# Strassen operands of the gates queued behind the last head's norm, two pools that wait tile by tile, one sum on another engine, three tiles in other rooms

## The chip, the cores and the metric

The kernel runs on one core of one Trainium2 chip. The metric is the device time of one execution in microseconds (us). TensorE (PE) does the matmuls and the transposes, VectorE (DVE), ScalarE (ACT) and GpSimd (POOL) work on tiles beside it, SyncE (SP) issues most of the DMAs and ACT the rest. Each engine takes its instructions in a fixed order; a wait of one instruction holds everything behind it on that engine, and that goes for SP's DMAs too.

## The reference

One layer of an encoder over 1024 tokens of width 1024, in float32, cut to what matters here:

```python
h = rmsnorm(x, g_mix)
z = h @ w_in                              # pooling channels | q | k | v
y_pool = pool_mixer(u_pool, ...)          # four windows
y_attn = diff_attention(q, k, v, ...)     # 8 heads, two softmax maps each, then
                                          # o = head_rmsnorm(o, g_sub) * (1 - lambda_init)
gates = sigmoid(h @ w_gate + b_gate)      # 2 x 1024 columns
merged = gates[..., :D] * (y_pool @ w_branch_pool) + gates[..., D:] * (y_attn @ w_branch_attn)
x = x + merged @ w_out
h2 = rmsnorm(x, g_ffn)
x = x + square(relu(h2 @ w_up)) @ w_down
```

## The kernel before

Every float32 matmul is done as three matmuls (`mm3`) of operands that are split in a high and a low part of fp32r. `split` makes the two parts: a cast on ACT (L116) and a subtraction on DVE or POOL (L117). Most matmuls are 128x128 by 128x512.

**Order.** The program is written tile by tile, and a planner with a clock of its own puts each engine's instructions in order, those written first going first where several are ready by that clock. `tc.issue_after(ins)` keeps what is written in its block, on the engine of `ins` alone, behind `ins` on that engine; it adds no wait for `ins` to finish. Tiles come from pools; tiles of one tag share the pool's `bufs` rooms in turn. A pool opened where an earlier one lay waits by default until every tile of the earlier ones is done with; with `reuse_waits="tile"` each of its tiles waits for those that lay at its own place.

**The heads.** A pipeline of stages runs over 8 heads with 8 query tiles each. At the end of a head, `stage_norm` makes the row of factors `r` for the head's output norm: three DVE steps (L594 to L596), two on POOL (L597 a power, L598 a product), a transpose on PE (`trr`, L600), a copy on ACT, and a DMA to `r_dram`. Its small tiles lie in the pool `sp`, its PSUM bank in `ps_t`; both close behind the heads, with `ps_s` and `ps_o`.

**Behind the heads** the rest of the mixer follows:

- `vpool` (six rooms of 4 KB a partition, where `sp` lay) and `pb` (five PSUM banks, where `ps_s`, `ps_o` and `ps_t` lay) are opened. `bank` deals the eight PSUM banks in turn: three of `ps_z` and `ps_f`, then five of `pb`.
- The `comb` sums: the token operand `hT` is combined into Strassen-Winograd sums in place, on DVE (L827, L830), and split again.
- `bp`: the pooled branch's projection, 16 groups of 12 matmuls, two for each d; ACT copies each group's bank to `m` (L935), and `m` goes to `mp_dram`.
- `gate_rest(d)` for d from 3 to 7: the rest of the gates' products in Strassen-Winograd form. It is a generator with four steps. Its first step loads `gr` (8 raw tiles of weights) and `ga`, makes S1, S3 and S2 by three POOL sums (L827, L830), splits S2, S1, S3 and A22 on ACT and DVE, and loads `xz`. Its later steps are the products gA and gB. In the second, ACT copies gA to `uv` (L893) before the next product is added to the same bank. In the third, DVE adds A to `v[:, 0]`, POOL adds the two halves of `v` (`xz`, L827), and SP stores that and `uv` to `g_dram`. `xz` and `uv` share four rooms (tag `fw`).
- `gate_rest(3)` and `gate_rest(4)` take their first step within the bp loop, behind d = 3 and d = 5.
- `load_yT(d)` brings the attention output of head d back from `y_dram` (`ryT`) and its factors from `r_dram` (`rb`), multiplies the two on DVE (L925) and splits the product to `yT`. The rows 0 to 4 use rooms of `vpool`, the rows 5 to 7 the one room of the tag `mx`. `fr` (two rooms of 2 KB) holds the gates' raw operand `ga`, and later sums (`tmp`).
- `ba`: the attention branch's projection, over all eight `yT`; then the gates, the output projection and the second norm.

**The MLP.** Up: 16 pairs of column blocks, seven Strassen-Winograd products each (`up_pair`). X is a PSUM bank in which product 6 is followed by product 7, added to the same bank, so ACT must copy X to `U2` (L1216) between them. `U2` takes one of nine rooms of the pool `e1` (tag `ev`), as do most other results of a pair; these go to DRAM (`ud`) by DMA. The operand sums S1 to S4 take rooms of the tag `sm`, in `es`, `e20` or `e21` by the pair's number. Down: seven products (Da, Db) with operands read back from DRAM; the rooms of its weight loads lie, among others, where `pr21` and `e21` lay.

Of the kernel before, what the change touches and what calls it, by code (L numbers as in the profile page):

```python
# [54 lines left out]
def encoder_kernel(  # L55
# [58 lines left out]
    def split(hi, lo, src, lo_eng=None):  # L114

        nc.scalar.copy(hi, src)  # L116
        return (lo_eng or nc.vector).tensor_tensor(lo, src, f(hi), op=ALU.subtract)  # L117
# [17 lines left out]
    def fr_tile(shape, name):  # L135
        return fp.tile(shape, F32, tag="fr", name=name, bufs=N_FR)
# [136 lines left out]
    with ExitStack() as ph:  # L273
# [116 lines left out]
        Zs = {}  # L390
        SS = {}

        gghs, z_last = {}, {}


        sq = sp.tile([P, 4, HD + 1], F32, name="sq")
# [192 lines left out]
        def stage_norm(h):  # L589

            rz = sp.tile([P, NT], F32, tag="rz", name=f"rz{h}")
            r = sp.tile([P, NT], F32, tag="r", name=f"r{h}")
            nc.vector.reciprocal(rz, Zs[h][:, 0, :])
            nc.vector.tensor_tensor(r, SS[h], rz, op=ALU.mult)  # L594
            nc.vector.tensor_tensor(r, r, rz, op=ALU.mult)
            nc.vector.tensor_scalar(r, r, 1.0 / P, EPS, op0=ALU.mult, op1=ALU.add)  # L596
            nc.gpsimd.tensor_tensor(r, r, mhalf, op=ALU.pow)  # L597
            nc.gpsimd.tensor_tensor(r, r, rz, op=ALU.mult)  # L598
            tr = ps_t.tile([P, 512], F32, tag="tr", name=f"trr{h}")
            nc.tensor.transpose(tr[0:NT, 0:P], r, identf)  # L600
            rT = sp.tile([NT, P], F32, tag="rT", name=f"rT{h}")
            nc.scalar.copy(rT, tr[0:NT, 0:P])
            nc.scalar.dma_start(r_dram[h].rearrange("(t q) -> t q", q=P), rT)
            yield
# [191 lines left out]
        next(gen)  # L796


    vpool = attn.enter_context(tc.tile_pool(name="vpool", bufs=N_V))
    pb = mix.enter_context(tc.tile_pool(name="pb", bufs=5, space=PSUM))  # L800
    nbank = [0]

    def vt(shape, dt, name):
        return vpool.tile(shape, dt, tag="V", name=name)
# [21 lines left out]
    def add(eng, out_, a, b):  # L826
        return eng.tensor_tensor(out_, a, b, op=ALU.add)  # L827
# [44 lines left out]
    def gate_rest(d):  # L872
        ds_ = slice(d * P, (d + 1) * P)
        r2 = raw([P, NK, P], f"gr{d}")
        nc.sync.dma_start(r2, w_gate[:, D + d * P : D + (d + 1) * P].rearrange("(kk p) c -> p kk c", p=P))
        r21, r22 = r2[:, 0:4, :], r2[:, 4:8, :]
        r11 = gate_raw(11, d)
        s1 = fo_tile(f"s1_{d}")[:, 0:512].rearrange("p (a b) -> p a b", a=4)
        add(pool, s1, r21, r22)
        sub(pool, r21, r11, r21)  # L880
        sub(pool, r11, s1, r11)
        ws = []
        for name, rw in (("S2", r11), ("S1", s1), ("S3", r21), ("A22", r22)):
            w = wt([P, 2, 4, P], f"{name}_{d}")
            split_made[d] = split(w[:, 0], w[:, 1], rw)
            ws.append(w)
        v = fw_tile([P, 2, 512], f"xz{d}", F32)
        nc.sync.dma_start(v, xz[ds_])
        u = fw_tile([P, 2, 512], f"uv{d}", F32)
        yield  # L890
        A, B = bank(f"gA_{d}"), bank(f"gB_{d}")
        gate_mm(A, ws[0], 2, True, True)
        nc.scalar.copy(u[:, 0, :], A)  # L893
        add(dve, u[:, 0, :], u[:, 0, :], v[:, 0, :])
        yield
        gate_mm(B, ws[2], 3, True, True)
        nc.scalar.copy(u[:, 1, :], B)
        gate_mm(A, ws[1], 1, False, True, True)
        add(dve, v[:, 0, :], A, v[:, 0, :])
        add(pool, v[:, 1, :], v[:, 0, :], v[:, 1, :])  # L900
        nc.sync.dma_start(g_dram[ds_, 512:S], v[:, 1, :])
        add(dve, u[:, 1, :], u[:, 1, :], v[:, 0, :])
        nc.sync.dma_start(g_dram[D + d * P : D + (d + 1) * P, 512:S], u[:, 1, :])
        yield
        gate_mm(B, ws[3], 4, False, True, True)
        add(dve, u[:, 0, :], B, u[:, 0, :])
        nc.sync.dma_start(g_dram[D + d * P : D + (d + 1) * P, 0:512], u[:, 0, :])
        yield
# [3 lines left out]
    def load_yT(d):  # L912

        rb = fu_tile(f"rb{d}") if d % 2 else ut([P, S], F32, f"rb{d}")
        nc.sync.dma_start(rb, r_dram[d].partition_broadcast(P))
        if d < N_YU:
            rw = vt([P, S], F32, f"ryT{d}")
        else:
            rw = fq.tile([P, S], F32, tag="mx", name=f"ryT{d}")
        nc.sync.dma_start(rw, y_dram[d * P : (d + 1) * P, :])  # L920
        ts = []
        for th in range(2):
            hs = slice(th * 512, (th + 1) * 512)
            t = yt_tile(d)([P, 2, 512], F32R, f"yT{d}_{th}", th)
            dve.scalar_tensor_tensor(rw[:, hs], rw[:, hs], gs, rb[:, hs], op0=ALU.mult, op1=ALU.mult)  # L925
            split(t[:, 0, :], t[:, 1, :], rw[:, hs])
            ts.append(t)
        yT.append(ts)

    gens = [gate_rest(d) for d in range(G_PLAIN, NK)]  # L930
    for d in range(NK):
        m = ut([P, S], F32, f"m{d}")
        for th in range(2):
            ps = proj_T(bank(f"bp{d}_{th}"), ws_bp[d - d % 2][d % 2], lambda k, th: pair(ypT[k][th]), th, nk=4)
            nc.scalar.copy(m[:, th * 512 : (th + 1) * 512], ps)  # L935
        nc.scalar.dma_start(mp_dram[d * P : (d + 1) * P, :], m)

        if d in (3, 5):
            next(gens[d // 2 - 1])

    NG = len(gens)
    for i in range(NG + 1):
# [167 lines left out]
    def ev(name, shape=(P, 512)):  # L1110
        return e1.tile(list(shape), F32, tag="ev", name=name)
# [62 lines left out]
    def up_pair(p):  # L1174
        cols_p = w_up[:, p * 2 * P : (p + 1) * 2 * P].rearrange("(kk p) (i c) -> i p kk c", p=P, i=2)

        def load(i, pool_):
            r = pool_.tile([P, NK, P], F32, tag="rw", name=f"wu{p}_{i}")
            nc.sync.dma_start(r, cols_p[i])
            return {f"{i + 1}{j + 1}": r[:, 4 * j : 4 * j + 4, :] for j in range(2)}  # L1180

        A = load(0, pr1)
        X = bx.tile([P, 512], F32, tag="X", name=f"X{p}", bufs=4)
        Y = (bm if p % 2 else bx).tile([P, 512], F32, tag="Y", name=f"Y{p}")
        u_product(X, "1", a_op(p, "11", A["11"], dve))
# [12 lines left out]
        def store(name, src, queue=nc.sync):  # L1198
            queue.dma_start(ud[name, p // 2][:, p % 2, :], src)

        finish("11", Y, x1)
        store("11", C["11"], nc.scalar)
        yield
        A.update(load(1, pr2[p % 3 > 0]))
        yield
        S1, S2, S3, S4 = (
            (e2[1] if p % 3 and p != 1 else e2[0] if i > 2 else es).tile(
                [P, 4, P], F32, tag="sm", name=f"s{i}_{p}"
            )
            for i in range(1, 5)  # L1210
        )
        add(dve, S1, A["21"], A["22"])
        sub(dve, S2, S1, A["11"])
        u_product(X, "6", a_op(p, "S2", S2, dve))
        U2 = ev(f"U2_{p}")
        nc.scalar.copy(U2, X)  # L1216
        zp, zt, zb = (bx, "X", 4) if p % 2 else (bm, "Z", 1)
        Z = zp.tile([P, 512], F32, tag=zt, name=f"Z{p}", bufs=zb)
        u_product(Z, "5", a_op(p, "S1", S1, dve))
        z5 = ev(f"z5_{p}")  # L1220
        nc.scalar.copy(z5, Z)
        sub(dve, S3, A["11"], A["21"])
        u_product(X, "7", a_op(p, "S3", S3, dve))
        U3 = ev(f"U3_{p}")
        nc.scalar.copy(U3, X)
        finish("22", X, z5)
        store("22", C["22"], nc.scalar)
        W = bm.tile([P, 512], F32, tag="W", name=f"W{p}")
        u_product(W, "4", a_op(p, "22", A["22"], dve))
        finish("21", W, U3)  # L1230
        store("12", C["21"], nc.scalar)
        sub(dve, S4, A["12"], S2)
        u_product(Z, "3", a_op(p, "S4", S4, dve))
        finish("12", Z, U2)

        s1 = ev(f"us1_{p}")
        add(dve, s1, C["12"], C["22"])
        store("S1", s1)
        s2 = ev(f"us2_{p}")
        sub(dve, s2, s1, C["11"])  # L1240
# [224 lines left out]
```

## Time and profile before

| | before |
|---|---|
| median of 3 runs | 1565.0 us (1563.77 to 1567.16) |
| the profiled execution | 1566.65 us, span 1564.8 us, granted clock 0.996 |
| PE busy | 1534.5 us (98%) |
| DVE, ACT, POOL busy | 992.4, 824.6, 401.5 us |
| DMA | 223.97 MB, mean 143 GB/s |

Rows of a timeline give start and duration in us, engine, line, operation, the tiles written and read with buffer numbers left out, shapes and count; in brackets stands how long the engine sat idle before it and what ended that. PE's ends are modelled, so the pace of matmuls is read from start to start. "PEclk" is the share of the full clock that was granted to PE. In the chain of waits each row is one piece of the work that ended last, and "issue" is time in which nothing that the profile shows was waited for.

### The profile page before, as it was taken

How to read it: one execution, taken by the hardware profiler on the slowest of the kernel's cores; microseconds unless marked ns; L12 is line 12 of the kernel's file. 1: busy time of each engine (PE TensorE's matmuls, PEld its weight loads, DVE VectorE, ACT ScalarE, POOL GpSimd, SP SyncE). 2: the span in 40 equal slices, each digit the busy share in tenths (PEclk: the TensorE clock that was granted, in tenths of full speed). 3: DMA queues.
4: the chain of work that ended last, by engine and by line, in shares of the span. 5: the costliest groups of instructions: out<-in, count | busy, mean ns of one | idle time of the engine just before them, and what ended most of it. 6: DMA issues, size and time to landing. Idle time of an engine off the chain costs nothing.

```text
span 1564.8 us, 21964 instructions
## 1 busy us (share of the span) xinstructions
PE 1534.5 (98%) x7653; PEld 1319.8 (84%) x7653; DVE 992.4 (63%) x1986; ACT 824.6 (53%) x1828; POOL 401.5 (26%) x484
## 2 busy tenths in 40 slices
PE   7999999999999999899999999999999999999998
PEld 6999999989999988777788887888888788888887
DVE  6666677676767765748542448866565668556662
ACT  6656566656576665344442547565555634333331
POOL 5525253535463451315545400000000000000000
PEclk9999999999999999999999999999999999999999
DMA  7202021212131123276766633554342789537650
GB/s 228 63 25 85 32 82 43 71 45 73 49 94 62 58 71 107 90 243 216 274 221 199 197 110 123 187 178 165 128 141 108 275 297 376 194 121 254 223 188 27
DMA packets 177544, 223.97 MB, mean 143 GB/s; under 512 B 10565, under 2 KB 111130, under 8 KB 177434
## 3 DMA queue, kind: packets, MB, share of 16 engines
q1 hardware_dynamic: 159594, 192.39, 37.7%
q10 hardware_dynamic: 17840, 30.19, 5.2%
q8 instruction: 60, 0.98, 0.3%
q14 instruction: 50, 0.41, 0.1%
HBM read 161.16 MB, written 61.37 MB: 142 GB/s over the span
## 4 chain that ended last, share of the span: by engine, by line
PE 85%; DVE 5%; DMA 4%; ACT 2%; issue 1%; POOL 1%; SPq 1%; ACTq 0%; DVEq 0%; POOLq 0%
PE z L122 5%; PE z L123 5%; PE z L124 5%; PE Da L123 4%; PE Da L122 4%; PE Da L124 4%; PE Db L123 3%; PE Db L122 3%; PE Db L124 3%; PE X L124 3%; PE X L122 3%; PE X L123 2%; PE sc L492 2%; PE sc L493 2%; PE op L124 2%; PE op L122 2%
## 5 line engine op out<-in xcount | busy, mean ns | idle before, releaser
L122 PE MATMUL z<-wqkv,hT 128*128 128x384 f32 x512 | 175.2, 343 | 0.3 <-DVE qn L436 0.2
L123 PE MATMUL z<-wqkv,hT 128*128 128x384 f32 x512 | 174.5, 342 | 0.4 <-POOL wqkv L117 0.4
L124 PE MATMUL z<-wqkv,hT 128*128 128x384 f32 x512 | 174.3, 341 | 0.4 <-DVE hT L117 0.3
L503 ACT ACTIVATE s<-s,nm 128x256 f32<-128x256 f32 (+7 forms) x128 | 99.7, 779 | 50.4 <-DVE nm L495 48.2
L433 POOL TENSOR_TENSOR ms<-ms,mhalf 128x4 f32<-128x4 f32 x64 | 68.6, 1073 | 135.2 <-DVE ms L431 135.0
L122 PEld LDWEIGHTS z<-wqkv,hT 128*128 128x128 f32 x512 | 97.1, 190 | 3.4 <-DVE qn L436 0.7
L124 PEld LDWEIGHTS z<-wqkv,hT 128*128 128x128 f32 x512 | 97.0, 190 | 3.5 <-DVE hT L117 1.2
L123 PEld LDWEIGHTS z<-wqkv,hT 128*128 128x128 f32 x512 | 97.2, 190 | 3.2 <-POOL wqkv L117 0.7
L495 DVE CUSTOM_DVE_ANT_0 s<-sc,dist 128x512 f32<-128x512 f32 (+3 forms) x128 | 74.8, 586 | 25.5 <-PE sc L493 22.9
L492 PE MATMUL sc<-K,Q 128*128 128x512 f32 (+2 forms) x192 | 68.5, 361 | 0.9 <-ACT oS L574 0.4
L493 PE MATMUL sc<-K,Q 128*128 128x512 f32 (+2 forms) x192 | 66.8, 355 | 0.0
L117 DVE TENSOR_TENSOR AS<-s,AS 128x512 fp32r<-128x512 f32 x64 | 43.7, 686 | 35.5 <-ACT AS L116 35.3
L117 POOL TENSOR_TENSOR wqkv<-rqkv,wqkv 128x384 fp32r<-128x384 f32 x60 | 62.9, 1067 | 8.8 <-ACT wqkv L116 4.7
L442 POOL TENSOR_TENSOR qn<-qn,ggh 128x128 f32<-128x128 f32 x64 | 31.4, 490 | 86.7 <-DVE qn L436 79.2
L123 PE MATMUL ba<-yT,wba 128*128 128x512 f32 x128 | 50.7, 396 | 1.1 <-DVE yT L117 1.1
L465 DVE TENSOR_TENSOR Q<-tk,Q 64x128 fp32r<-64x128 f32 x128 | 36.6, 286 | 22.7 <-ACT Q L464 20.9
L124 PE MATMUL ba<-yT,wba 128*128 128x512 f32 x128 | 50.6, 395 | 0.0
L122 PE MATMUL ba<-yT,wba 128*128 128x512 f32 x128 | 50.6, 395 | 0.0
L122 PE MATMUL op<-wo,mT 128*128 128x512 f32 x128 | 50.2, 396 | 0.0
L466 ACT CAST Q<-tk 64x128 fp32r<-64x128 f32 x128 | 33.2, 260 | 32.3 <-DVE Q L465 30.1
L123 PE MATMUL op<-wo,mT 128*128 128x512 f32 x128 | 50.2, 394 | 0.0
L124 PE MATMUL op<-wo,mT 128*128 128x512 f32 x128 | 50.1, 393 | 0.0
(489 smaller groups left out, 4796.1 us busy)
## 6 DMA issues: line engine op xcount, KB each, us to landing
wd<-in_w_down_dram SPq DMA_DIRECT2D x56, 512.0 KB, 5.5
wu<-in_w_up_dram SPq DMA_DIRECT2D x32, 512.0 KB, 4.7
udS<-us SPq DMA_DIRECT2D x64, 256.0 KB, 2.1
ur<-udS SPq DMA_DIRECT2D x32, 512.0 KB, 4.0
rqkv<-in_w_in_dram SPq DMA_DIRECT2D x64, 192.0 KB, 2.7
ud<-u ACTq DMA_DIRECT2D x48, 256.0 KB, 2.1
ur<-ud SPq DMA_DIRECT2D x24, 512.0 KB, 4.2
ga<-in_w_gate_dram SPq DMA_DIRECT2D x25, 256.0 KB, 2.8
```

Of the source, the lines that this page charges most:

```text
L117: return (lo_eng or nc.vector).tensor_tensor(lo, src, f(hi), op=ALU.subtract)
L122: nc.tensor.matmul(ps, lhs_hi, rhs_hi, start=first, stop=False, **kw)
L123: nc.tensor.matmul(ps, lhs_hi, rhs_lo, start=False, stop=False, **kw)
L124: return nc.tensor.matmul(ps, lhs_lo, rhs_hi, start=False, stop=last, **kw)
L433: nc.gpsimd.tensor_tensor(ms, ms, mhalf[:, 0:4], op=ALU.pow)
L442: nc.gpsimd.tensor_tensor(qn[:, 2:4, :], qn[:, 2:4, :], ggh.unsqueeze(1).broadcast_to([P, 2, HD]), op=ALU.mult)
L465: nc.vector.tensor_tensor(Q[own, m, 1, :], q, f(q_hi), op=ALU.subtract)
L466: nc.scalar.copy(Q[other, m, 1, :], q)
L492: nc.tensor.matmul(dst, Q[:, i, 0, :], rhs, start=True, stop=False)
L493: nc.tensor.matmul(dst, Q[:, i, 1, :], rhs, start=False, stop=True)
L495: nc.vector.tensor_tensor_reduce(out=s[i][:, c : c + w], in0=sc[:, 0:w], in1=dist[:, o0 + c : o0 + c + w], scale=2.0 ** -(h + 1), scalar=B ...
L503: nc.scalar.activation(s[i][:, 0:n], s[i][:, 0:n], AF.Exp, bias=last, scale=-1.0, accum_out=Z[:, i, t : t + 1])
```

## The change

- The DVE and POOL instructions of the first steps of `gate_rest(3)` and `gate_rest(4)` stand behind the last head's L596 on DVE and its L598 on POOL.
- `vpool` and `pb` wait tile by tile.
- The sum of the two halves of `v` in `gate_rest` runs on DVE.
- `load_yT(7)` loads its row as two halves into the two rooms of `fr`, by two DMAs, in place of the `mx` room.
- `U2` of the last pair (15) takes a room of `e21`, whose tiles were last the operand sums of pair 14.

```diff
-        gghs, z_last = {}, {}
+        gghs, z_last, normed = {}, {}, {}
...
-            nc.vector.tensor_scalar(r, r, 1.0 / P, EPS, op0=ALU.mult, op1=ALU.add)
+            normed[h] = [nc.vector.tensor_scalar(r, r, 1.0 / P, EPS, op0=ALU.mult, op1=ALU.add)]
             nc.gpsimd.tensor_tensor(r, r, mhalf, op=ALU.pow)
-            nc.gpsimd.tensor_tensor(r, r, rz, op=ALU.mult)
+            normed[h].append(nc.gpsimd.tensor_tensor(r, r, rz, op=ALU.mult))
...
-    vpool = attn.enter_context(tc.tile_pool(name="vpool", bufs=N_V))
-    pb = mix.enter_context(tc.tile_pool(name="pb", bufs=5, space=PSUM))
+    vpool = attn.enter_context(tc.tile_pool(name="vpool", bufs=N_V, reuse_waits="tile"))
+    pb = mix.enter_context(tc.tile_pool(name="pb", bufs=5, space=PSUM, reuse_waits="tile"))
...
-        add(pool, v[:, 1, :], v[:, 0, :], v[:, 1, :])
+        add(dve, v[:, 1, :], v[:, 0, :], v[:, 1, :])
...
-        if d < N_YU:
-            rw = vt([P, S], F32, f"ryT{d}")
+        if d == NK - 1:
+
+            rws = [fr_tile([P, 512], f"ryT{d}_{th}") for th in range(2)]
+            for th in range(2):
+                nc.sync.dma_start(rws[th], y_dram[d * P : (d + 1) * P, th * 512 : (th + 1) * 512])
         else:
-            rw = fq.tile([P, S], F32, tag="mx", name=f"ryT{d}")
-        nc.sync.dma_start(rw, y_dram[d * P : (d + 1) * P, :])
+            if d < N_YU:
+                rw = vt([P, S], F32, f"ryT{d}")
+            else:
+                rw = fq.tile([P, S], F32, tag="mx", name=f"ryT{d}")
+            nc.sync.dma_start(rw, y_dram[d * P : (d + 1) * P, :])
+            rws = [rw[:, 0:512], rw[:, 512:S]]
...
         if d in (3, 5):
-            next(gens[d // 2 - 1])
+            with ExitStack() as later:
+                for ins in normed[H - 1]:
+                    later.enter_context(tc.issue_after(ins.ins))
+                next(gens[d // 2 - 1])
...
-        U2 = ev(f"U2_{p}")
+
+        U2 = ev(f"U2_{p}") if p < NP - 1 else e2[1].tile([P, 512], F32, tag="sm", name=f"U2_{p}")
```

More of the change, by code (lines that the diff above doesn't have):

```diff
@@ L915, in load_yT @@
         nc.sync.dma_start(rb, r_dram[d].partition_broadcast(P))
-        if d < N_YU:
-            rw = vt([P, S], F32, f"ryT{d}")
-        else:
-            rw = fq.tile([P, S], F32, tag="mx", name=f"ryT{d}")
-        nc.sync.dma_start(rw, y_dram[d * P : (d + 1) * P, :])
+        if d == NK - 1:
+            rws = [fr_tile([P, 512], f"ryT{d}_{th}") for th in range(2)]
+            for th in range(2):
+                nc.sync.dma_start(rws[th], y_dram[d * P : (d + 1) * P, th * 512 : (th + 1) * 512])
+        else:
+            if d < N_YU:
[4 more added lines that the diff above has]
+            rws = [rw[:, 0:512], rw[:, 512:S]]
         ts = []
-        for th in range(2):
-            hs = slice(th * 512, (th + 1) * 512)
+        for th, r in enumerate(rws):
             t = yt_tile(d)([P, 2, 512], F32R, f"yT{d}_{th}", th)
-            dve.scalar_tensor_tensor(rw[:, hs], rw[:, hs], gs, rb[:, hs], op0=ALU.mult, op1=ALU.mult)
-            split(t[:, 0, :], t[:, 1, :], rw[:, hs])
+            dve.scalar_tensor_tensor(
+                r, r, gs, rb[:, th * 512 : (th + 1) * 512], op0=ALU.mult, op1=ALU.mult
+            )
+            split(t[:, 0, :], t[:, 1, :], r)
             ts.append(t)
```

## The prediction

> **What bounds the kernel now.** I read the page's busy shares first, then TensorE's waits, then the stretches around the longest of them, then single rows. TensorE (PE) is the bound:
>
> ```profile
> span 1564.8 us, 21964 instructions
> PE 1534.5 (98%) x7653; PEld 1319.8 (84%) x7653; DVE 992.4 (63%) x1986; ACT 824.6 (53%) x1828; POOL 401.5 (26%) x484
> ```
>
> The matmuls stay the same, so only PE's 30.3 us of idle and its slow stretches can go. The list of waits says where they are (engine, tile and line that waited, on whom: us in total, times, longest). Besides one at the start, which the diff doesn't touch, these are the long ones:
>
> ```profile
> PE trr L600 <- POOL r L598: 4.0, 1, 4.0
> PE X L122 <- ACT U L1216: 2.5, 2, 1.9
> PE gA L122 <- ACT uv L893: 2.3, 1, 2.3
> PE bp L122 <- ACT m L935: 1.9, 1, 1.9
> ...
> PE ba L123 <- DVE yT L117: 1.1, 1, 1.1
> ```
>
> The diff can reach all five. Two have a tail in the clock. Stretches (length, busy time of PE, PEld, DVE, ACT and POOL with counts, then PEclk, DMA share, GB/s) and PE's rows show it:
>
> ```profile
> 666.60:672.70 6.10, 6.09 (x15) 4.79 (x16) 4.95 (x5) 2.66 (x4) 0.00 (x0) 0.51 0.70 254
> ...
> 1243.80:1249.50 5.70, 3.83 (x10) 2.94 (x10) 4.96 (x6) 4.34 (x6) 0.00 (x0) 0.70 1.04 402
> ```
>
> ```profile
> 665.89 0.37 PE L600 MATMUL trr<-identf,r 128*8 128x128 f32 x1 [3.96 <-POOL r L598]
> 666.61 0.80 PE L122 MATMUL bp<-ypT,wbp 128*128 128x512 f32 x1 [0.34 <-ACT rT L602]
> ...
> 672.65 0.39 PE L124 MATMUL bp<-ypT,wbp 128*128 128x512 f32 x1
> 672.88 0.39 PE L122 MATMUL bp<-ypT,wbp 128*128 128x512 f32 x1
> ```
>
> The full pace is 0.23 us a matmul (672.65 to 672.88). After the last head's norm the clock is 0.51 for 6 us: 6.10 - 15 x 0.23 = 2.7 lost there, on top of 3.96 + 0.34 idle; the norm costs 7.0. In U2's stretch 5.70 - 10 x 0.23 = 3.4 are lost, 1.9 of it the wait and 1.5 the slow clock.
>
> The Trainium skill, "TensorE: Matmul & The Clock Gate", Part 1, has the clock at half after an idle window of about 3.4 us and back after as long a busy one. By that the norm's tail is half of 3.4, an estimate of 1.7, and a stall of 1.9 us has none; the trace disagrees on both (2.7 and 1.5), and the sum below would be 2.5 us less by the rule.
>
> **The change part by part.**
>
> **Operands behind the norm; pools tile by tile.** Why the norm is late:
>
> ```profile
> 650.48 1.27 DVE L594 TENSOR_TENSOR r<-SS,rz 128x8 f32<-128x8 f32 x1
> ...
> 652.81 1.21 DVE L117 TENSOR_TENSOR hT<-combe,hT 128x1024 fp32r<-128x1024 f32 x1
> ...
> 658.37 1.09 DVE L117 TENSOR_TENSOR S<-ga,S 128x512 fp32r<-128x512 f32 x1 [3.15 <-ACT S L116]
> ...
> 662.75 0.16 DVE L596 TENSOR_SCALAR r<-r 128x8 f32<-128x8 f32 x1
> ```
>
> ```profile
> 647.45 4.28 POOL L827 TENSOR_TENSOR s<-gr 128x512 f32<-128x512 f32 x1 [31.71 <-DMA gr<-in_w_gate_dram]
> ...
> 662.98 2.55 POOL L597 TENSOR_TENSOR r<-r,mhalf 128x8 f32<-128x8 f32 x1 [2.38 <-DVE r L596]
> ...
> 685.09 1.43 POOL L827 TENSOR_TENSOR s<-gr 128x512 f32<-128x512 f32 x1 [19.25 <-DMA gr<-in_w_gate_dram]
> ```
>
> ```profile
> 657.72 0.62 ACT L116 CAST S<-ga 128x512 fp32r<-128x512 f32 x1 [6.60 <-POOL ga L830]
> ...
> 658.24 0.58 ACT L935 COPY m<-bp 128x512 f32<-128x512 f32 x1
> ```
>
> GpSimd (POOL) adds gate operands first; ScalarE's (ACT) cast waits 6.60 us for them, with the copy that empties a bp bank right behind it, which is the bp wait; VectorE's (DVE) subtraction waits for the cast, and the norm's L596 stands behind that. The change puts the DVE and POOL instructions of both moved steps behind L596 and L598. How long the chain takes then, and where PE meets it:
>
> ```profile
> L597 POOL TENSOR_TENSOR r<-r,mhalf x8: 1636/1638/2551, 139.5 to 663.0; 128x8 f32<-128x8 f32 x8
> ```
>
> ```profile
> 642.43 0.40 PE L122 MATMUL bp<-ypT,wbp 128*128 128x512 f32 x1
> ```
>
> L594 at 650.5; a small step takes 0.2 where POOL is off (below); with two sums of DVE, 1.2 each (652.81), between dependent steps L595 comes at 653.1 and L596 at 655.7; then 0.2, 1.64 for the power and 0.2: the transpose can run at 657.7. On PE the transpose stands behind six groups of twelve bp matmuls that begin at 642.43; 72 x 0.23 = 16.6, and 0.4 for sums of squares between: 659.4 without waits. There is no wait then, unless the planner now puts the transpose ahead of some groups. Bounds: 0 (place kept), and with two groups less, 5.5 sooner, 657.7 - 653.9 = 3.8. I take 1.0, nearer to the place that the row shows: 6.0 of 7.0 gone.
>
> Of the moved steps everything issues as before: in each two loads on SP (gr, ga) and the xz load, three POOL sums, four casts on ACT, four subtractions on DVE. Loads and casts get no new edge. POOL's six sums start at 657.7 instead of 647.45; behind them POOL has nothing until the next gate's sums at 685.09. Behind the cast stand the bp copies, as before; what hides them is eight PSUM banks in place of the three that PE used until the norm was out (six groups, two to a bank, stood ahead of it): a copy may be seven groups late, 19 us. If the banks didn't come free tile by tile, the bp wait would stay: bounds 0 and 1.9, I take 1.9. The rooms of ryT come free sooner as well; now their loads start right behind the norm's store:
>
> ```profile
> 666.59 0.29 ACTq L603 DMA_DIRECT2D r_dram<-rT  x1
> ```
>
> ```profile
> 668.67 1.76 SPq L920 DMA_DIRECT2D ryT<-y_dram  x4
> ```
>
> Earlier ryT loads cost nothing, since now they run beside the bp matmuls at a DMA share of 0.70 and PE waits for none. Who is late next is the first gate matmul:
>
> ```profile
> 697.28 0.39 PE L122 MATMUL gA<-hT,S 128*128 128x512 f32 x1
> ```
>
> It comes 1.9 + 6.0 = 7.9 sooner, at 689.4. POOL's fourth sum is its operand: four sums at 1.43 to 4.28 end at 663.4 to 674.8, cast and subtraction at 665 to 676; DVE's eight left sums and splits of hT, 1.2 each, may stand behind: 675 to 686, still ahead. Bounds 0 and 6 (the second rival); I take 0.9.
>
> **One sum on DVE; the last row in two rooms.** The chain that ended last:
>
> ```profile
> 727.44 0.61 DVE xz L827
> ...
> 728.12 4.10 POOL xz L827
> ...
> 732.23 2.38 DMA g_dram<-xz
> ...
> 734.71 0.59 ACT uv L893
> ...
> 741.00 5.67 DMA ryT<-y_dram
> ```
>
> The POOL sum holds a store on SP, the store the room of the next copy, that copy PE: the wait of 2.3. On DVE the sum takes 0.61 and comes at once or some two sums later (DVE runs without a gap here), so the store goes 2.2 to 3.4 us sooner; bounds 0.1 left and none, and DVE's queue may grow by the two sums ahead of this, 1.2. I take 1.9 of 2.3. In all it is 5 x 0.61 = 3.1 more on DVE, spread over a stage of 60 us, and five sums less on POOL.
>
> The ryT of the last row waits in the one mx room for the row before it (741.00). In two fr rooms, free once the gates' raw operands are split, it loads before that, by two DMAs instead of one on SP. What is next there is DVE's own queue, without the load's 5.67, five times the wait. Bounds 0 and 1.1; I take 1.1.
>
> **U2 of the last pair.**
>
> ```profile
> 1237.67 7.41 DMA ud<-u
> ...
> 1245.15 0.59 ACT U L1216
> ```
>
> The copy waits for a store to leave its room. The new room held an operand sum of the pair before, which was split before that pair's last product. The whole 3.4 goes if the next product's operands are there; bounds 0 and 3.4, I take 3.4, since the wait names nothing else.
>
> **Sum.** 1.9 + 6.0 - 0.9 + 1.9 + 1.1 + 3.4 = 13.4. The profiled execution took 1566.65 (the span and 1.85 around it), 1.65 above the median; 1566.65 - 13.4 = 1553.2, on the median's scale 1565.0 - 13.4 = 1551.6. With all five stalls gone, 1.9 + 7.0 + 2.3 + 1.1 + 3.4 = 15.7: 1549.3.
>
> **The rivals.** *The norm's stall moves.* The planner puts the transpose two groups ahead: 3.8 idle and a tail of 2.7 stay, 0.5 of 7.0 gone instead of 6.0: 13.4 - 5.5 = 7.9, 1557. For it: the place was set by the planner's own clock, which expected POOL sooner than it came. Against: in the list of waits trr appears once, so the seven heads before made PE wait for nothing.
>
> *POOL and DVE slow each other at the gate operands.* A 128x8 step of the norm took 1.27 beside POOL's sum against a median of 0.17, POOL's sum 4.28 against 1.43 later. Six POOL sums now fall wholly on DVE's sums of hT: four at 4.28 end at 674.8, and eight of DVE at 2.3 behind the subtraction end at 676 + 18.4 = 694.4. PE, due at 689.4, waits 5 and has a tail of 1.5: 13.4 + 0.9 - 6.5 = 7.8, 1557.
>
> ```profile
> L594 DVE TENSOR_TENSOR r<-SS,rz x8: 148/169/1270, 138.9 to 650.5; 128x8 f32<-128x8 f32 x8
> ```
>
> ```profile
> 659.38 2.31 DVE L830 TENSOR_TENSOR combc<-combb,comba 128x1024 f32<-128x1024 f32 x1
> ```
>
> The Trainium skill, "SBUF — State Buffer", "Who interferes with whom", has the rule: a VectorE instruction with two SBUF inputs contends with a GpSimd one that reads SBUF, and the later one "fully blocks". By that rule, which the trace bears out (1.27 against 0.17), POOL's later start speaks against the change and the sum's move to VectorE for it.
>
> *Slower: an early ryT load blocks SP.* With rooms free tile by tile the planner may put ryT loads ahead of the last two ypT loads on SP:
>
> ```profile
> 623.69 6.45 SPq L185 DMA_DIRECT2D rypT<-p_dram  x2
> ```
>
> If one stands there for the room that the norm's row leaves (stored at 666.59, free at 668.67; with the transpose at 657.7 free at 660), SP holds ypT and the gate loads, and bp starts at 663 at the soonest instead of 642.4: 20.6 idle, a tail of 2.7, less 13.4: 9.9 slower, 1575. It decides when bp starts later than 642.4 + 13.4 - 2.7 + 3.1 = 656. Against: the planner plans these rooms' releases itself.
>
> *Nothing net.* Each wait has another right behind it: DVE's queue at the gates, another store at U2. 1563.
>
> **How the numbers follow.** The sum 0.62 (own range 1547 to 1555), the norm's stall moves 0.14, POOL and DVE 0.12, nothing net 0.06, slower 0.06. 0.2% is 3.1 us, about what can be told from no change. Faster is 0.62 + 0.14 + 0.12 = 0.88, same 0.06, slower 0.06. The range 1546 to 1559 leaves out the last two and some edges of the first three.
>
> **What would show it.** Right: trr's wait under 2 us and no clock of 0.51 behind it; bp groups not broken off after six before the transpose; gA's first row near 689; no wait of gA on uv or of ba on yT above 0.5; X of the last pair without a wait, and the first Da matmul some 13 us sooner. Wrong: a long wait of PE at 642 (ypT), at the first gA, or in the down phase's first steps, whose weight rooms lie where U2 now stays.

## The result, and the profile after

The changed kernel takes 1556.2 us in the median of six runs (1553.64 to 1559.58), against 1564.58 of the kernel before, measured beside it (1562.94 to 1567.16): a ratio of 0.9946, interval 0.9931 to 0.996, so 8.4 us faster (6.3 to 10.8). Measured once more, beside the last experiments, it came to 0.9936 (0.9923 to 0.9948), 1555.4 against 1565.64. The profiled execution took 1556.86, with a span 10.1 us shorter than before. The head of the page of the changed kernel, span and busy shares:

```profile
span 1554.7 us, 21968 instructions
...
PE 1529.8 (98%) x7653; PEld 1315.5 (85%) x7653; DVE 990.4 (64%) x1991; ACT 824.9 (53%) x1828; POOL 390.7 (25%) x479
```

TensorE's waits in the changed kernel (engine, tile and line, on whom: us in total, times, longest):

```profile
PE gA L122 <- ACT uv L893: 3.2, 3, 1.7
PE trr L600 <- POOL r L598: 1.6, 1, 1.6
PE gA L122 <- ACT u L699: 1.6, 1, 1.6
...
PE X L122 <- ACT U L1228: 0.7, 1, 0.7
```

Of the five waits that the diff could reach, three are gone: bp on m, ba on yT, and the 1.9 of X in the last pair. The 0.7 that is left of X is an earlier one (961.38, in the kernel before 968.42), which stood in the 2.5 of before as well; its line, the copy to `U2`, is L1228 in the changed kernel. The wait of trr is down from 4.0 to 1.6, and gA on uv has grown from 2.3 in one wait to 3.2 in three. Behind the norm the clock stays whole. The same stretch of the changed kernel, from the last bp matmul before the transpose (length, busy time of PE, PEld, DVE, ACT and POOL, PEclk, DMA share, GB/s), and PE's rows in it:

```profile
660.17:672.70 12.53, 10.92 (x48) 8.59 (x47) 8.51 (x6) 5.03 (x8) 12.33 (x8) 1.00 0.76 264
```

```profile
643.22 0.40 PE L122 MATMUL bp<-ypT,wbp 128*128 128x512 f32 x1
...
660.17 0.39 PE L124 MATMUL bp<-ypT,wbp 128*128 128x512 f32 x1
662.16 0.27 PE L600 MATMUL trr<-identf,r 128*8 128x128 f32 x1 [1.61 <-POOL r L598]
662.19 0.48 PE L122 MATMUL bp<-ypT,wbp 128*128 128x512 f32 x1
...
690.16 0.39 PE L122 MATMUL gA<-hT,S 128*128 128x512 f32 x1
```

The sum is best checked by stages, since PE runs them one behind the other. The table has the time between first matmuls, read from the timeline of each profiled execution: from bp to the first gA behind it (the norm), to the first op of the output projection (gates and ba), to Da (the rest of the mixer and MLP up), to the end (down). These are single executions; the medians stand in the experiments.

| kernel | bp at | bp to gA | gA to op | op to Da | Da to end |
|---|---|---|---|---|---|
| before | 642.43 | 54.85 | 148.10 | 407.60 | 311.9 |
| after | 643.22 | 46.94 | 148.18 | 404.20 | 312.2 |
| after, measured again | 642.27 | 46.94 | 147.21 | 403.73 | 312.2 |
| norm's part alone | 641.72 | 49.20 | 150.67 | 405.43 | 311.9 |
| pools' part alone | 642.54 | 52.99 | 148.59 | 405.39 | 311.9 |
| U2's part alone | 641.17 | 54.59 | 149.24 | 403.94 | 312.5 |
| after, sum on POOL | 642.03 | 46.94 | 150.36 | 404.07 | 312.5 |
| after, mx room | 642.21 | 46.94 | 148.46 | 403.79 | 312.3 |
| after, norm's power alone | 642.86 | 45.17 | 145.88 | 403.71 | 313.1 |
| the same, U2 in es | 642.67 | 45.17 | 146.97 | 403.74 | 312.4 |

The first stage gave 7.91 us and the third 3.40, as much as the prediction's terms for them (7.9 and 3.4). The gates gave nothing (148.10 to 148.18), where 2.1 net were expected; 0.8 was lost ahead of bp, where the diff does nothing, and 0.35 in the down phase: 7.9 - 0.1 + 3.4 - 0.35 - 0.8 = 10.05, the 10.1 by which the span is shorter.

### The profile page after: what moved, and what is told of

It reads as the page before. It is cut to its first block, busy times and chain, and to the rows that moved or that the text cites. A ratio compares the mean times of both kernels' runs of the same rounds, so it can differ in the third digit from the quotient of the medians.

```text
span 1554.7 us, 21968 instructions
## 1 busy us (share of the span) xinstructions
PE 1529.8 (98%) x7653; PEld 1315.5 (85%) x7653; DVE 990.4 (64%) x1991; ACT 824.9 (53%) x1828; POOL 390.7 (25%) x479
## 4 chain that ended last, share of the span: by engine, by line
PE 50%; DMA 1%; DVE 1%; ACT 0%; issue 0%; ACTq 0%; DVEq 0%
PE Da L123 4%; PE Da L122 4%; PE Da L124 3%; PE Db L123 3%; PE Db L124 3%; PE Db L122 3%; PE X L124 3%; PE X L123 3%; PE X L122 3%; PE op L124 2%; PE op L123 2%; PE op L122 2%; PE ba L124 2%; PE ba L123 2%; PE ba L122 2%; PE Z L124 2%
## 5 line engine op out<-in xcount | busy, mean ns | idle before, releaser
L495 DVE CUSTOM_DVE_ANT_0 s<-sc,dist 128x512 f32<-128x512 f32 (+3 forms) x128 | 74.8, 586 | 24.5 <-PE sc L493 22.6
L117 POOL TENSOR_TENSOR wqkv<-rqkv,wqkv 128x384 fp32r<-128x384 f32 x60 | 62.3, 1058 | 10.1 <-ACT wqkv L116 6.9
L466 ACT CAST Q<-tk 64x128 fp32r<-64x128 f32 x128 | 33.3, 260 | 32.1 <-DVE Q L465 30.0
L464 ACT CAST Q<-tk 64x128 fp32r<-64x128 f32 x128 | 33.1, 259 | 32.3 <-DVE K L463 30.1
L122 PE MATMUL op<-wo,mT 128*128 128x512 f32 x128 | 50.2, 396 | 0.0
L123 PE MATMUL op<-wo,mT 128*128 128x512 f32 x128 | 50.2, 394 | 0.0
```

Of the source, the lines that this page charges most:

```text
L122: nc.tensor.matmul(ps, lhs_hi, rhs_hi, start=first, stop=False, **kw)
L123: nc.tensor.matmul(ps, lhs_hi, rhs_lo, start=False, stop=False, **kw)
L464: nc.scalar.copy(q_hi, q)
L466: nc.scalar.copy(Q[other, m, 1, :], q)
L495: nc.vector.tensor_tensor_reduce(out=s[i][:, c : c + w], in0=sc[:, 0:w], in1=dist[:, o0 + c : o0 + c + w], scale=2.0 ** -(h + 1), scalar=B ...
```

## The experiments

Three questions were open: which part carries the gain; why the gates' stage gives nothing; and what the remaining waits are.

**Each large part alone, on the kernel before.** First the operands behind the norm:

```diff
...
-            next(gens[d // 2 - 1])
+            with ExitStack() as later:
+                for ins in normed[H - 1]:
+                    later.enter_context(tc.issue_after(ins.ins))
+                next(gens[d // 2 - 1])
```

> The kernel before with the first part alone: the first steps of gate_rest(3) and (4) behind the last head's norm on DVE and POOL; the pools still wait as a whole. Theory A (the norm is late only because it stands behind the operands' subtraction on DVE): L596 comes near 656, trr's wait falls from 4.0 to under 2.5, no stretch at half clock follows, the wait of bp on m (1.9) is gone; about 7 us faster, ratio 0.9955. Rival B (PE has only three banks until the norm is out, so it runs dry there whatever the norm does): trr or the first bp behind it still waits 4 us or more, 2 us faster at most.

Measured: 1559.93 against 1565.73, 0.9957 (0.9944 to 0.9969). Its waits on PE:

```profile
PE gA L122 <- ACT uv L893: 2.3, 1, 2.3
PE X L122 <- ACT U L1219: 2.0, 2, 1.4
...
PE trr L600 <- POOL r L598: 1.6, 1, 1.6
PE ba L123 <- DVE yT L117: 1.1, 1, 1.1
```

The order behind the norm carries most of the gain. The wait of bp on m is gone as well, though the banks still wait for whole pools: taking the gate's cast from in front of the copies was enough, and the eight banks that the prediction named as their cover weren't needed. The transpose waits 1.6 as in the changed kernel, and bp 0.3 for the copy of rT behind it, which it doesn't in the changed kernel (662.16 to 662.19), where the banks wait tile by tile. Here a slow clock follows, against the theory, and bp to gA takes 49.20 in place of 46.94 (one stretch of this kernel):

```profile
662.80:668.80 6.00, 6.00 (x21) 4.68 (x21) 5.83 (x3) 2.32 (x3) 6.00 (x4) 0.74 0.86 271
```

Next, the pools alone:

```diff
-    vpool = attn.enter_context(tc.tile_pool(name="vpool", bufs=N_V))
-    pb = mix.enter_context(tc.tile_pool(name="pb", bufs=5, space=PSUM))
+    vpool = attn.enter_context(tc.tile_pool(name="vpool", bufs=N_V, reuse_waits="tile"))
+    pb = mix.enter_context(tc.tile_pool(name="pb", bufs=5, space=PSUM, reuse_waits="tile"))
```

> The kernel before with the second part alone: vpool and pb wait tile by tile, the norm still behind the operands. Theory A: the norm is as late as before and the transpose stands where the planner's clock puts it, so trr still waits about 4 us with a slow tail; only the wait of bp (1.9) can go; 0 to 2 us faster, ratio 0.999 to 1. Rival B (the banks were the cause): PE runs more bp groups before the transpose, trr's wait is under 1, 7 us faster.

Measured: 1563.66, 0.9986 (0.9976 to 0.9995). Its waits:

```profile
PE trr L600 <- POOL r L598: 2.4, 1, 2.4
PE gA L122 <- ACT uv L893: 2.3, 1, 2.3
PE X L122 <- ACT U L1216: 2.0, 2, 1.4
PE bp L122 <- ACT m L935: 1.9, 1, 1.9
```

Small, but not nothing: ba's wait is gone, trr's is shorter, bp's is there unchanged. Rival B is refuted, but theory A isn't borne out in its details either: it had trr at 4, and bp's wait as the one that could go. Why trr waits less here no run shows. And the U2 room alone:

```diff
-        U2 = ev(f"U2_{p}")
+        U2 = ev(f"U2_{p}") if p < NP - 1 else e2[1].tile([P, 512], F32, tag="sm", name=f"U2_{p}")
```

> The kernel before with U2 of the last pair in the other room, alone. The prediction's term: X's wait of 1.9 near 1245 and the slow clock behind it are gone, 3.4 to 3.6 us faster, ratio 0.9978. Rival: the weight loads of the down phase, whose rooms lie there, come later and PE waits at the first Da or Db products: less than 1 us faster.

Measured: 1563.37, 0.9985 (0.9976 to 0.9993), 2.4 us, between what the term and the rival had. X on L1216 waits 0.7 once instead of 2.5; trr, bp, gA and ba wait as before. In the two kernels above, which leave U2 where it was, the stage from op to Da takes 405.4, not 407.6 as in the profiled execution of before: that execution's stall was longer (1.9 against 1.4) and had a slow tail that these have not. Against 405.4, U2's move is worth 1.5 there.

The three alone make 5.80 + 2.07 + 2.36 = 10.2 against the kernel before, measured beside them, about as much as the whole change (8.4 and 10.2). The other two parts should then be worth about nothing, which two kernels took back one at a time.

**The sum back on POOL**, the rest as in the changed kernel:

```diff
-        add(dve, v[:, 1, :], v[:, 0, :], v[:, 1, :])
+        add(pool, v[:, 1, :], v[:, 0, :], v[:, 1, :])
```

> The changed kernel with the sum of the halves of v back on POOL (undoes the third part). Prediction's step (the sum on DVE shortens the chain store, room, copy of gA): the waits of gA on uv grow from 3.2 by about 2, 1 to 2 us slower than the changed kernel. Theory C (the sum's place in DVE's full queue and the store's 5 to 7 us to landing are what PE waits for, the sum's engine hardly matters): the waits stay within 1 us of 3.2 and the time within 1 us of the changed kernel's.

Measured: 1556.6 against 1565.73, 0.9936 (0.9923 to 0.9949), which can't be told from the changed kernel. The times on the way of the first three gates show why. xz (A) is DVE's sum of gA to `v[:, 0]`, the sum is that of the two halves, and the last column is the whole way from the end of the first to the copy that PE waits for:

| kernel | xz (A) ends | sum ends | store issued | next copy to uv | whole way |
|---|---|---|---|---|---|
| before | 710.70, 728.04, 741.58 | 712.45, 732.20, 743.84 | 713.50, 732.23, 743.86 | 718.13, 734.71, 750.23 | 7.43, 6.67, 8.65 |
| after | 704.29, 723.59, 735.39 | 708.02, 724.79, 736.49 | 708.04, 724.82, 738.14 | 715.01, 729.63, 743.17 | 10.72, 6.04, 7.78 |
| sum on POOL | 703.23, 720.58, 736.61 | 704.98, 724.74, 740.12 | 706.03, 724.76, 740.15 | 710.54, 727.72, 744.62 | 7.31, 7.14, 8.01 |

The whole way is 22.8, 24.5 and 22.5 us in all. (The third copy of the kernel before shows no wait for its store: ACT was busy until then.) On DVE the first sum stands in a queue. DVE's rows of the changed kernel, then the copy and the store that it waits for:

```profile
703.61 0.69 DVE L827 TENSOR_TENSOR xz<-gA,xz 128x512 f32<-128x512 f32 x1
704.21 0.68 DVE L117 TENSOR_TENSOR S<-gr,S 128x512 fp32r<-128x512 f32 x1
704.80 0.68 DVE L117 TENSOR_TENSOR A<-gr,A 128x512 fp32r<-128x512 f32 x1
705.41 1.41 DVE L931 SCALAR_TENSOR_TENSOR ryT<-ryT,gs,rb 128x512 f32<-128x512 f32 x2
706.73 0.68 DVE L117 TENSOR_TENSOR yT<-ryT,yT 128x512 fp32r<-128x512 f32 x1
707.34 0.68 DVE L827 TENSOR_TENSOR xz<-xz 128x512 f32<-128x512 f32 x1
```

```profile
715.01 0.59 ACT L893 COPY uv<-gA 128x512 f32<-128x512 f32 x1 [4.92 <-DMA g_dram<-xz]
```

```profile
708.04 0.32 SPq L901 DMA_DIRECT2D g_dram<-xz  x1
```

```profile
738.14 4.95 DMA g_dram<-xz
```

Five other instructions stand ahead of the sum, so that it ends 3.73 after xz (A), on POOL 1.75. From the store to the copy it then takes 7.0, 4.8 and 5.0 us, and before 4.6, 2.5 and 6.4; the prediction priced this step on the 2.5 alone. What PE pays is in the list of the kernel with the sum on POOL:

```profile
PE gA L122 <- ACT uv L893: 4.0, 2, 3.3
```

There it waits 3.29 for the second copy (the one that the prediction priced) and 0.75 for the third; with the sum on DVE 0.37, 1.06 and 1.74 for the three. The second wait falls by 2.2, and 1.4 comes back at the other two. In single executions the stage is 2.2 and 3.2 shorter with the sum on DVE (150.36 against 148.18 and 147.21), of which the waits are 0.8 and 1.7 (4.0 against 3.2 and 2.3) and most of the rest a slow stretch behind the 3.29; in the medians nothing is left that can be told.

**The last row back in the mx room:**

```diff
-        if d == NK - 1:
+        if False:
```

> The changed kernel with the last row of yT again in the one mx room (undoes the fourth part). Prediction's step: the wait of ba on yT (1.1) is back, about 1 us slower than the changed kernel. Rival D (early ryT loads lie ahead of the stores in the DMA engines): the stores of the sums land sooner (under 4 us instead of 4.7 to 7), the waits of gA on uv fall by 1 or more, and the time is the same or better.

Measured: 1555.85 against 1565.19, 0.9943 (0.9931 to 0.9955), not to be told from the changed kernel either. What ba got back gA gave (its waits):

```profile
PE ba L123 <- DVE yT L117: 1.6, 1, 1.6
...
PE gA L122 <- ACT uv L893: 1.2, 2, 0.8
```

So the two rooms do take away ba's wait of 1.6, and gA's waits go from 1.2 to 3.2 with it (2.3 when the changed kernel was measured again): with ba's stall ahead of it, PE waits 0.75 for the copy of the third of these gates (745.00, its store at 740.58) in place of 1.74, and nothing for the second's in place of 1.06. Rival D had the stores land sooner, and that came only in part: from store to copy the first two take 7.6 and 3.7 us here, in place of 7.0 and 4.8.

**DVE's rows of yT behind the sums.** If the queue on DVE is what holds the sum, the products and splits of later rows can be put behind it:

```diff
...
-        add(dve, v[:, 1, :], v[:, 0, :], v[:, 1, :])
+        halves_sum[d] = add(dve, v[:, 1, :], v[:, 0, :], v[:, 1, :])
...
-                load_yT(d)
+                with ExitStack() as later:
+                    if d > 1:
+                        later.enter_context(tc.issue_after(halves_sum[G_PLAIN + max(i - 2, 0)].ins))
+                    load_yT(d)
```

> The changed kernel with one more order on DVE: load_yT(2) and (3) behind the sum of the halves of v of gate 3, load_yT(4) and (5) behind that of gate 4, load_yT(6) and (7) behind that of gate 5. Theory C (each of the three waits of gA on uv is a room that a store leaves late, because the sum stands behind rows of yT in DVE's full queue): the sums of gates 4 and 5 come 5 us or more sooner after the last matmul that they read, all three waits fall under 0.3, 3 to 4 us faster than the changed kernel (1552 to 1553). Rival D (the store's landing of 5 to 7 us beside the loads is what counts): stores still land that slowly and at least 1.5 of the 3.2 stay. Rival E: the rows of yT come too late and ba waits in their place, no gain.

Measured: 1558.82, 0.9961 (0.9948 to 0.9975), no faster than the changed kernel (0.9946 and 0.9936). The gates got better, another stage worse. Two of the three waits on uv went, as theory C has it, and one of 1.7 stays behind a store that is 6.7 us from its copy, as rival D has it; rival E's wait of ba doesn't show. Its waits:

```profile
PE op L122 <- ACT wo L116: 3.2, 2, 2.4
...
PE gA L122 <- ACT uv L893: 1.7, 1, 1.7
...
PE op L123 <- POOL wo L117: 0.9, 1, 0.9
```

gA to op takes 146.20, 2.0 less than after, but op to Da 408.67, 4.5 more: the planner now begins a row of three raw loads of `w_out` 8.2 us ahead of the first op matmul (827.47 to 835.67) instead of 15.8 (822.52 to 838.34), so that it ends behind that matmul, and op waits for the splits. An order that mends the gates' waits is dear where the same queues carry the next stage's loads.

**The load of xz later.** In the program of either kernel uv4 lies where xz3 lay, uv5 where xz4 and uv6 where xz5, because the load of xz, a gate ahead, takes the room that is free. This kernel loads it behind ACT's copy of gA, for the gates from 5 on:

```diff
-        v = fw_tile([P, 2, 512], f"xz{d}", F32)
-        nc.sync.dma_start(v, xz[ds_])
+        if d < 5:
+            v = fw_tile([P, 2, 512], f"xz{d}", F32)
+            nc.sync.dma_start(v, xz[ds_])
...
         nc.scalar.copy(u[:, 0, :], A)
+        if d >= 5:
+            v = fw_tile([P, 2, 512], f"xz{d}", F32)
+            nc.sync.dma_start(v, xz[ds_])
```

> The changed kernel, with the load of xz for the gates from 5 on written behind ACT's copy of gA, so that uv takes the room that is free and the load waits for the store. Theory (the copy to uv waits only because the load of xz a gate ahead took the free room): the gA waits of about 3.2 us fall under 0.5, about 3 us faster than the changed kernel. Rival (the sum in VectorE's queue is what is late, and the rooms only pass it on): VectorE or the next product waits for the later xz load instead, and the time stays within 1 us of the changed kernel's.

Measured: 1563.9 against 1565.64, 0.9987 (0.9978 to 0.9996), so 8 us slower than the changed kernel. Its waits, and one of DVE's rows:

```profile
PE op L122 <- ACT wo L116: 3.6, 2, 2.4
PE gA L122 <- ACT uv L894: 2.4, 1, 2.4
...
PE gB L122 <- ACT uv L901: 1.0, 1, 1.0
PE op L123 <- POOL wo L117: 0.9, 1, 0.9
```

```profile
746.37 0.69 DVE L827 TENSOR_TENSOR uv<-uv,xz 128x512 f32<-128x512 f32 x1 [4.38 <-DMA xz<-xz]
```

The gates 3 to 6 run without a wait (707.82 to 740.49), so the room is what held them. But both theories' signs are there: DVE waits for the late xz, the last gate waits 2.4 and 1.0, and the three loads of `w_out` begin 8.2 us ahead of op, as in the run before. The stage from op to Da takes 410.70, 7.0 more than in the changed kernel measured beside it; another 2.3 is lost ahead of bp, which starts at 644.54, and no run says why. So the wait is one of room, and neither of the two orders that were tried to shorten it pays.

**The norm's power without DVE beside it.** The changed kernel's transpose still waits 1.6. DVE's and POOL's rows of it:

```profile
653.61 0.16 DVE L595 TENSOR_TENSOR r<-r,rz 128x8 f32<-128x8 f32 x1
653.69 1.22 DVE L830 TENSOR_TENSOR combc<-combb,comba 128x1024 f32<-128x1024 f32 x1
...
655.96 0.16 DVE L596 TENSOR_SCALAR r<-r 128x8 f32<-128x8 f32 x1
656.04 1.22 DVE L830 TENSOR_TENSOR comba<-comba,hT 128x1024 f32<-128x1024 f32 x1
657.17 1.22 DVE L117 TENSOR_TENSOR hT<-combc,hT 128x1024 fp32r<-128x1024 f32 x1
```

```profile
656.21 4.81 POOL L597 TENSOR_TENSOR r<-r,mhalf 128x8 f32<-128x8 f32 x1 [39.69 <-DVE r L596]
661.10 1.01 POOL L598 TENSOR_TENSOR r<-r,rz 128x8 f32<-128x8 f32 x1
```

L596 came at 656.0, 0.3 from where the prediction had it. But the power took 4.81 where its median was 1.64, with DVE's sums of `hT` running beside it at 1.22 each. In this kernel the last head's product by `rz` goes to DVE, and the second half of the sums of `hT` stands behind it (the gates' operands on POOL now stand behind the power):

```diff
...
-            nc.gpsimd.tensor_tensor(r, r, mhalf, op=ALU.pow)
-            normed[h].append(nc.gpsimd.tensor_tensor(r, r, rz, op=ALU.mult))
+            normed[h].append(nc.gpsimd.tensor_tensor(r, r, mhalf, op=ALU.pow))
+            if h < H - 1:
+                nc.gpsimd.tensor_tensor(r, r, rz, op=ALU.mult)
+            else:
+                normed[h][0] = nc.vector.tensor_tensor(r, r, rz, op=ALU.mult)
...
+        with ExitStack() as later:
+            if kp:
+                later.enter_context(tc.issue_after(normed[H - 1][0].ins))
...
```

> The changed kernel with the last head's norm freed of DVE's company: its last product r*rz on DVE instead of POOL, and the second half of the comb sums (from the first subtraction of hT on, kp = 1) behind that product on DVE. Theory F (the power on POOL took 4.81 instead of 1.64 and the product 1.01 instead of 0.20 because DVE's sums with two SBUF operands run beside them): the power takes 1.7 or less, trr's wait of 1.6 is gone, 1.5 us faster than the changed kernel if the comb sums, 2 us later, hold nothing up. Rival: the power stays above 3 us and trr waits as before.

Measured: 1553.74 against 1565.19, 0.9931 (0.9918 to 0.9943). POOL's row and what DVE pays:

```profile
654.70 1.64 POOL L597 TENSOR_TENSOR r<-r,mhalf 128x8 f32<-128x8 f32 x1 [38.54 <-DVE r L596]
```

```profile
656.37 1.24 DVE L601 TENSOR_TENSOR r<-r,rz 128x8 f32<-128x8 f32 x1 [1.75 <-POOL r L597]
...
660.91 2.31 DVE L117 TENSOR_TENSOR hT<-combc,hT 128x1024 fp32r<-128x1024 f32 x1
```

The power is back at 1.64, trr waits for nothing, and bp to gA takes 45.17 instead of 46.94. This settles the rest of the norm's stall: it was POOL's two steps beside DVE (the product had taken 1.01 against a median of 0.20), not the place of the transpose, which still stands behind six groups.

**U2 in another room.** Where U2 lies in `e21`, the six first weight loads of the down phase are split: before, all six go at 1218.62 to 1226.97; after, two at 1215.94 and 1216.98 and four at 1238.30 to 1243.46. The kernel just shown has the wait that follows from it:

```profile
1281.51 1.04 ACT L116 CAST w_0h<-wd 128x1024 fp32r<-128x1024 f32 x1 [4.42 <-DMA wd<-in_w_down_dram]
```

```profile
1282.61 1.21 PE L122 MATMUL Db<-w_0h,u_0h 128*128 128x512 f32 x4 [0.88 <-ACT w_0h L116]
```

The next one is the same with U2 in `es`:

```diff
-        U2 = ... else e2[1].tile([P, 512], F32, tag="sm", name=f"U2_{p}")
+        U2 = ... else es.tile([P, 512], F32, tag="sm", name=f"U2_{p}")
```

> The changed kernel with the last product of the norm on VectorE and the second half of the sums of hT behind it (as in the run before it of that kind, 1553.7), and U2 of the last pair in a room of es instead of e21. Theory (U2 in e21 holds back the weight loads of the down phase whose rooms lie there, and Db waits for their cast): the weight loads are issued before the last pair's end again, the wait of Db on w_0h goes, 1 to 1.5 us faster than with e21, about 9.5 to 12 below before. Rival (those loads are late for another cause): the wait of about 0.9 stays and the time is the same.

Measured: 1553.26 against 1565.64, 0.9926 (0.9912 to 0.994). The six loads go at 1207.97 to 1216.56 again, and Db waits for nothing:

```profile
1283.28 1.08 PE L122 MATMUL Db<-w_0h,u_0h 128*128 128x512 f32 x4
```

Da to the end falls from 313.1 to 312.4, as the cause asks; but Da waits 0.5 on an operand and the gates took 1.1 more in this execution, and in the medians 0.5 us isn't to be told from nothing. This is the fastest version measured, though not by more than the noise.

**The changed kernel again, and all three together.**

> The changed kernel once more, beside the next three on the same chip. Expected: about 8 us faster than before, gA waiting on the copies to uv for about 3 us in three waits, Db waiting on the cast w_0h for about 0.6 us. If the waits of gA come out elsewhere or with other lengths, their sizes are chance and the room theory of the next runs is weakened.

Measured: 1555.4, 0.9936 (0.9923 to 0.9948). gA waits on uv 2.3 in two waits, Db 0.3: two of the three places come back, the first doesn't, and the whole changes by a microsecond. By what was expected before the run, the sizes of these waits are in part chance, and the theory of the rooms rests on the late load of xz, where the waits of the gates 4 to 6 went, not on sizes.

> The norm's product on VectorE, U2 in es, and the late load of xz together. If the three causes (POOL's power slowed by VectorE's sums, the free room taken early, the weight loads held back) are separate, their gains add: trr, gA on uv and Db on w_0h each wait under 0.5, and the time is about 1549 to 1551, 14 to 16 below before. If they share a cause or one wait takes another's place, it is no faster than the better of the two runs before it.

Measured: 1559.67, 0.9963 (0.9949 to 0.9976). The late xz takes away more than the others bring: op waits 3.4 on `wo` in all, gA still 2.0 and gB 1.9.

The last run was to have a fifth room for xz and uv:

> The version of 1553.3 (norm's product on VectorE, U2 in es), with five rooms in place of four for the tag fw, in which xz and uv lie; nothing else. Theory (a copy to uv waits because its room is the one that the store of xz has yet to leave): with a fifth room it takes one that is free, the gA waits on uv of 2.2 us fall under 0.5, and the time is about 1551, 14 below before. Rival (the gates' chain is late at another place, as when xz was loaded late: VectorE's queue, loads behind stores on SyncE): the wait moves to xz, gB or the operands of the output projection, and the time is within 1 us of 1553.3 or above it.

The kernel that ran still had four, so it repeats the version with U2 in `es`, and whether a fifth room pays wasn't tried. It measured 1554.7, 0.9932 (0.9918 to 0.9946), with 2.6 of waits of gA on uv against 2.2: two measurements of one program, 1.4 us apart.

## Why the prediction was right, and where it was not

- **The norm and bp, 1.9 + 6.0 = 7.9: right in its mechanism, and in its number by some luck.** bp to gA became 7.91 shorter. The first gA row stands at 690.16 for 689.4, with bp 0.8 later. But the stage takes 45.17 where PE waits for nothing (the norm's power alone), so before it lost 54.85 - 45.17 = 9.7, where the sum had 7.0 + 1.9 = 8.9, and the changed kernel still loses 1.8, where the sum left 1.0. The two misses of 0.8 cancel. Part of the first lies in how a wait is read: the list counts from the modelled end of the matmul ahead, 0.39 after its start, while at full pace the next one starts after 0.23. The second has a reason that the term did not have: a 4.81 us power in place of the 1.64 that it was given. The prediction's second rival had the mechanism, POOL and DVE slowing each other, but saw it at the gate sums and not at the power. The Trainium skill, "SBUF — State Buffer", "Who interferes with whom", has this rule for a VectorE instruction with two SBUF inputs beside a GpSimd one that reads SBUF. The trace bears it out at both places (4.81 against 1.64, and DVE's 2.31 against 1.2 beside the gate sums). Which of the two pays differs: the power was slowed while DVE's sums kept 1.22, and so was the POOL sum of 4.28 in the kernel before, beside DVE instructions of 1.21.
- **The tail of the clock: gone here as expected, but not something to count on.** After 1.61 of idle the changed kernel's clock stayed at 1.00; after 1.60 and 0.34 in the norm's part alone it was 0.74 for 6 us. The cleanest pair are two waits of gA on uv of 2.32 us each, the stretch behind it first with the pools' part alone, then with the norm's part alone:

```profile
733.70:739.70 6.00, 6.00 (x19) 4.76 (x20) 5.27 (x7) 4.11 (x7) 2.14 (x2) 0.72 0.69 227
```

```profile
729.10:735.10 6.00, 6.00 (x27) 4.96 (x28) 4.28 (x6) 3.44 (x7) 1.35 (x2) 1.00 0.52 168
```

  The one runs 19 matmuls in 6 us, the other 27. So the tails of 2.7 and 1.5 that the sum took from one execution are not owed to each stall of that length. Where a tail does come behind these shorter stalls, it has one size. PE's rows of the norm's part alone, where eight matmuls take 0.43 each, near half the pace, for 3.4 us:

```profile
662.54 0.62 PE L124 MATMUL bp<-ypT,wbp 128*128 128x512 f32 x1
662.97 0.63 PE L122 MATMUL bp<-ypT,wbp 128*128 128x512 f32 x1
...
665.95 0.41 PE L123 MATMUL bp<-ypT,wbp 128*128 128x512 f32 x1
```

  That loses 8 x 0.20 = 1.6, and so do the tails behind U2's stall before and behind gA's with the pools' part alone. What decides whether it comes stays open: no run was made for it. By the Trainium skill, "TensorE: Matmul & The Clock Gate", Part 1, an idle of this length has no tail, and the second stretch agrees while the first doesn't; the page also has the window run freely, so that it may fall differently from run to run, and whether that is the cause here no run shows.
- **The gate operands, -0.9: not needed.** POOL's six sums ended at 672.6, and the first gA ran without a break at 690.16. The casts waited and nobody waited for them. That bp's wait would go only with the banks tile by tile was wrong: it went with the order alone.
- **One sum on DVE, 1.9: the step that failed.** It priced one chain, the second gate's, with its landing of 2.38, and let the sum come "at once or some two sums later" in DVE's queue. At that gate the term is there: beside the same kernel with the sum on POOL, PE waits 1.06 in place of 3.29. (In the kernel before it was 2.30.) But the first gate's sum came five instructions later and its way took 10.72 in place of 7.43, and the third's lost the cover of ba's stall. PE now waits at all three: 3.2 in place of 2.3.
- **The last row in two rooms, 1.1: right at its place, paid at another.** ba's wait went. With the mx room back it is 1.6, and gA's waits 1.2 in place of 3.2 and 2.3. The prediction had named as next "DVE's own queue", and charged nothing for it.
- **U2, 3.4: right in this pair of executions, too large as a price.** op to Da fell by 3.40. Alone the part is worth 2.4 in the median, 1.5 of its stage against executions of the old room without the tail, and it gives 0.3 to 0.9 back in the down phase, the place that the prediction had named as a sign against it.
- **The rivals.** The two at 1557 didn't happen, though 1556.2 is nearer to them than to the sum: the transpose stayed behind its six groups, and the first gA waited for nothing. "Nothing net", each wait with another behind it, is what the gates alone show. SP was held by an early ryT load, as the slower rival had it, but when bp was already running (643.22), so that PE lost nothing. SP's row, five loads from the first to the last:

```profile
658.88 6.91 SPq L926 DMA_DIRECT2D ryT<-y_dram  x5
```

In sum: 13.4 expected, 10.1 in the profiled execution, 8.4 and 10.2 in the medians. What is missing is the gates' 2.1 above all, and in the medians a tail that U2's stall had in the profiled execution of before and not in others. The 1556.2 lies in the stated range (1546 to 1559) and just outside that of the sum alone (1547 to 1555): the causes of the gain were right, its size too large by 3 to 5.

## What to carry to other kernels

A queue order that keeps work of a stage that isn't due off an engine is worth much where a short dependent chain stands behind it, and it is worth asking what the freed engines now do beside that chain. A step that only passes a room on (sum, store, landing, copy) should be priced over all its repetitions, not the one that waited: the others have slack only as long as the stall in front stays. When a wait is mended by reordering, look at what the same queue loads for the next stage, since two mends of the gates came back as waits of the output projection.

## What the runs showed of the hardware

A 128x8 power on POOL took 4.81 us beside DVE's two-operand 128x1024 sums and 1.64 without them, while the sums kept their 1.22. Beside POOL's 128x512 sums, DVE's 128x1024 instructions took 2.31 instead of 1.21. The other way round, a 128x512 sum on POOL took 4.28 beside DVE's that kept 1.21. Two stalls of 2.32 us at one place were followed by clocks of 0.72 and of 1.00 over 6 us; the slow part was 3.4 us of matmuls at 0.43 in place of 0.23. The way from a store's issue to the copy that waits for its room took 2.5 to 7.0 us within one stage of two kernels.
